# Weighted sum over experts: nine ring slots in chunks of three, one token of each chunk summed by TensorE in a loop, the code of three engines placed at instruction slot 128

## The chip, the cores and the metric

The kernel runs on one core of a Trainium2 chip. The metric is the device time of one execution in microseconds (us); lower is better. Before the change the median of three runs is 707.68 us, from 707.18 to 707.82.

A core has five engines with instruction queues of their own: TensorE (PE; its weight loads are listed apart as PEld), VectorE (DVE), ScalarE (ACT), GpSimd (POOL) and SyncE (SP). They meet only at semaphores. Transfers between the device memory and SBUF, the on-chip memory of 128 partitions, run on sixteen DMA engines; SP's DMAs stand in queue q1, ScalarE's in q10.

## The reference

```python
def setup_inputs():
    batch, seq, n_experts, expert_dim = 16, 1024, 8, 512
    return {
        "expert_outputs": np.random.randn(batch, seq, n_experts, expert_dim).astype(np.float32),
        "combine_weights": np.random.randn(batch, seq, n_experts).astype(np.float32),
    }

def reference(expert_outputs, combine_weights):
    weights = combine_weights[..., np.newaxis]
    return np.sum(expert_outputs * weights, axis=2).astype(np.float32)
```

Each of 16384 tokens has eight rows of 512 floats and eight weights; its output is the weighted sum of its rows. 268.4 MB are loaded and 33.6 MB stored, and each loaded value is used once.

## The kernel before

**Layout.** Tokens are spread over the 128 partitions, 128 tokens to a partition. "A token" in what follows means one token on every partition: 16 KB per partition or 2.097 MB to load, 2 KB per partition or 0.262 MB to store. 120 of the 128 go through a loop, in twelve rounds of ten; the last eight (the tail) go through code of their own.

**Buffers.** `ring` has ten token slots, filled in chunks of 4, 4 and 2 slots (`CHUNKS`). `acc` holds two halves of ten output tokens, one for even and one for odd rounds. `w_t` holds all weights, `w_c` those of two rounds.

**SP** (`loads_and_last_stores`) issues all loads of x (L101). A chunk of a round may be loaded again once `done`, a count of finished tokens, says that the chunk's tokens of the round before are summed (L99). The weights are loaded behind the first chunk (L105, L108). Behind the loop come eight loads of one tail token each (L111), then the last round's store (L91) and four stores of tail tokens of 4, 2, 1 and 1 tokens (L115).

**ScalarE** (`weights_and_stores`) issues the stores of the other rounds (L91), waits for each to land and then copies the weights of the round after next into `w_c` (L136). When the loop is over it writes diagonal matrices `diag`, the identity times one weight, for the tail (L143), five in flight.

**VectorE** (`terms`) does all sums of the loop. For a chunk it takes the semaphore `loaded` (L165), multiplies the first rows of all its tokens by their weights in one instruction (L189), then adds the other seven rows token by token in fused multiply-adds (L179), two tokens in turn, so that each instruction's wait on `step` for the one before it of the same token is covered by the other token's.

**TensorE** (`first_terms`) works only in the tail: for each of the eight tail tokens it sums the first four to six rows as products of a diagonal matrix with a row (L155), accumulating in PSUM; VectorE adds the remaining rows (L179 with `ps`), and for the last token both parts (L223, L230).

**GpSimd** writes the identity matrix at the start.

The order of the work is written out by hand: each engine runs its list in order, VectorE's loop of six iterations covers two rounds each, and no scheduler moves anything.

Of the kernel before, what the change touches and what calls it, by code (L numbers as in the profile page):

```python
# [10 lines left out]
def kernel(  # L11
# [17 lines left out]

    nc = tc.nc  # L30
    fp32 = mybir.dt.float32
    mult, add = mybir.AluOpType.mult, mybir.AluOpType.add

    B, S, E, D = expert_outputs.shape
    T = B * S
    P = 128
    R = 10
    G = 2 * R
    M = 2 * G
    T_P = T // P  # L40
    GROUPS = T_P // G
    LOOP = GROUPS * G
    TAIL = T_P - LOOP
    ROUNDS = LOOP // R
    CHUNKS = [(0, 4), (4, 4), (8, 2)]
    C = len(CHUNKS)
    DIAGS = 5

    x = expert_outputs.rearrange("b s e d -> (b s) e d")
    w = combine_weights.rearrange("b s e -> (b s) e")  # L50
    o = out.rearrange("b s d -> (b s) d")
    cut = LOOP * P
    x_g = x[0:cut].rearrange("(n p b g) e d -> n b p g e d", p=P, b=2, g=G)
    w_g = w[0:cut].rearrange("(n p m) e -> p n m e", p=P, m=M)
    o_g = o[0:cut].rearrange("(n p b g) d -> n b p g d", p=P, b=2, g=G)
    x_t = x[cut:T].rearrange("(p j) e d -> p j e d", j=TAIL)
    w_x = w[cut:T].rearrange("(p j) e -> p j e", j=TAIL)
    o_t = o[cut:T].rearrange("(p j) d -> p j d", j=TAIL)


    pe_e = [6, 6, 6, 6, 5, 5, 5, 4]
    tail_stores = [(0, 4), (4, 2), (6, 1), (7, 1)]
    diags = [(j, e) for j in range(TAIL) for e in range(pe_e[j])]
# [4 lines left out]
    acc = one.tile([P, G, D], fp32, name="acc")  # L68
    w_t = one.tile([P, T_P, E], fp32, name="w_t")
    w_c = one.tile([P, G, E], fp32, name="w_c")  # L70
    ident = one.tile([P, P], fp32, name="ident")
    diag = one.tile([P, DIAGS, P], fp32, name="diag")
    ps = psum.tile([P, TAIL, D], fp32, name="ps")

    sem = tc.alloc_semaphore
    w_in = sem("w_in")
    w_set = [sem(f"w_set{h}") for h in range(2)]
    loaded = [sem(f"loaded{c}") for c in range(C)]
    stored = [sem(f"stored{h}") for h in range(2)]
    step = sem("step")  # L80
    done = sem("done")
    tail_in = [sem(f"tail_in{j}") for j in range(TAIL)]
    tail_out = sem("tail_out")
    id_set = sem("id_set")
    diag_set = sem("diag_set")
    product = sem("product")

    def store(queue, n):
        h = n % 2
        queue.wait_ge(done, (n + 1) * R)  # L90
        queue.dma_start(  # L91
            out=o_g[n // 4, n // 2 % 2, :, h * R : h * R + R], in_=acc[:, h * R : h * R + R]
        ).then_inc(stored[h], 16)

    def loads_and_last_stores(sync):
        for n in range(ROUNDS):
            for c, (r, m) in enumerate(CHUNKS):
                if n:
                    sync.wait_ge(done, (n - 1) * R + r + m)  # L99
                g = n % 2 * R + r  # L100
                sync.dma_start(  # L101
                    out=ring[:, r : r + m], in_=x_g[n // 4, n // 2 % 2, :, g : g + m]
                ).then_inc(loaded[c], 16)
                if n == 0 and c == 0:
                    sync.dma_start(  # L105
                        out=w_t[:, 0:LOOP].rearrange("p (n m) e -> p n m e", m=M), in_=w_g
                    ).then_inc(w_in, 16)
                    sync.dma_start(out=w_t[:, LOOP:T_P], in_=w_x).then_inc(w_in, 16)  # L108
        for j in range(TAIL):
            sync.wait_ge(done, LOOP - R + j + 1)  # L110
            sync.dma_start(out=ring[:, j], in_=x_t[:, j]).then_inc(tail_in[j], 16)  # L111
        store(sync, ROUNDS - 1)
        for j, m in tail_stores:
            sync.wait_ge(done, LOOP + j + m)
            sync.dma_start(out=o_t[:, j : j + m], in_=acc[:, j : j + m]).then_inc(tail_out, 16)  # L115
# [13 lines left out]
    def weights_and_stores(scalar):  # L129
        scalar.wait_ge(w_in, 32)  # L130
        for n in range(ROUNDS):
            h = n % 2
            if n >= 2:
                store(scalar, n - 2)
                scalar.wait_ge(stored[h], 16 * (n // 2))
            scalar.copy(  # L136
                out=w_c[:, h * R : h * R + R], in_=w_t[:, n * R : n * R + R]
            ).then_inc(w_set[h], 1)
        store(scalar, ROUNDS - 2)
        scalar.wait_ge(stored[0], 16 * ROUNDS // 2)  # L140
        scalar.wait_ge(id_set, 2)
        for k, (j, e) in enumerate(diags):
            i = scalar.mul(out=diag[:, k % DIAGS], in_=ident, mul=w_t[:, LOOP + j, e : e + 1])  # L143
            i.then_inc(diag_set, 1)
            if k >= DIAGS:
                i.wait_op(product, k - DIAGS + 1, "sem-ge")
        scalar.wait_ge(stored[1], 16 * ROUNDS // 2)
        scalar.wait_ge(tail_out, 16 * len(tail_stores))

    def first_terms(tensor):  # L150
        for k, (j, e) in enumerate(diags):
            if e == 0:
                tensor.wait_ge(tail_in[j], 16)
            tensor.wait_ge(diag_set, k + 1)
            tensor.matmul(  # L155
                ps[:, j],
                lhsT=diag[:, k % DIAGS],
                rhs=ring[:, j, e],
                start=e == 0,
                stop=e == pe_e[j] - 1,  # L160
            ).then_inc(product, 1)

    def terms(vector):
        def take(s, v):
            vector.wait_ge(s, v).then_inc(s, -v)  # L165

        last = {}

        def count(i, g, e):

            if e == E - 1:
                i.then_inc(done, 1)
            else:
                i.then_inc(step, 1)
                last["all"] = last.get("all", 0) + 1
                last[g] = last["all"]

        def fused(g, e, weight, before):
            return vector.scalar_tensor_tensor(  # L179
                out=acc[:, g], in0=ring[:, g % R, e], scalar=weight, in1=before, op0=mult, op1=add  # L180
            )

        with nc.Fori(0, GROUPS, engines=OrderedEngineSet([vector.engine])):
            for h in range(2):
                take(w_set[h], 1)
                for c, (r, m) in enumerate(CHUNKS):
                    take(loaded[c], 16)
                    q = h * R + r
                    i = vector.tensor_tensor(  # L189
                        out=acc[:, q : q + m],  # L190
                        in0=ring[:, r : r + m, 0],
                        in1=w_c[:, q : q + m, 0:1].to_broadcast([P, m, D]),
                        op=mult,
                    )
                    i.then_inc(step, 1)
                    last["all"] = last.get("all", 0) + 1
                    last.update((g, last["all"]) for g in range(q, q + m))
                    for g in range(q, q + m, 2):
                        for e in range(1, E):
                            for k in (g, g + 1):  # L200
                                i = fused(k, e, w_c[:, k, e : e + 1], acc[:, k])
                                i.wait_op(step, last[k], "sem-ge")
                                count(i, k, e)
            take(step, last["all"])

        last.clear()
        for q in ((0, 1), (2,), (3,), (4,), (5,), (6,)):
            for e in range(pe_e[q[0]], E):
                for j in q:
                    weight = w_t[:, LOOP + j, e : e + 1]  # L210
                    if e == pe_e[j]:
                        i = fused(j, e, weight, ps[:, j])
                        i.wait_op(product, sum(pe_e[: j + 1]), "sem-ge")
                    else:
                        i = fused(j, e, weight, acc[:, j])
                        i.wait_op(step, last[j], "sem-ge")
                    count(i, j, e)

        j = TAIL - 1
        for e in range(pe_e[j], E):  # L220
            weight = w_t[:, LOOP + j, e : e + 1]
            if e == pe_e[j]:
                i = vector.tensor_scalar_mul(out=acc[:, j], in0=ring[:, j, e], scalar1=weight)  # L223
                i.wait_op(tail_in[j], 16, "sem-ge")
            else:
                i = fused(j, e, weight, acc[:, j])
                i.wait_op(step, last[j], "sem-ge")
            count(i, j, -1)
        vector.wait_ge(step, last[j])  # L229
        i = vector.tensor_tensor(out=acc[:, j], in0=acc[:, j], in1=ps[:, j], op=add)  # L230
        i.wait_op(product, len(diags), "sem-ge")
        count(i, j, E - 1)

    with tc.tile_critical(no_gpsimd_drain=True):  # L234
        loads_and_last_stores(nc.sync)
        identity(nc.gpsimd)
        weights_and_stores(nc.scalar)
        first_terms(nc.tensor)
        terms(nc.vector)
# [30 lines left out]
```

## Time and profile before

| | |
|---|---|
| median of three runs | 707.68 us |
| the profiled execution, its own time | 707.67 us |
| its span, first to last instruction | 705.5 us |
| granted TensorE clock, mean | 0.998 |
| moved by DMA | 302.53 MB, 429 GB/s over the span |
| VectorE busy | 642.8 us, 898 instructions |
| fused multiply-add, 128x512, with `w_c` | 840 of 745 ns each, which overlap a little |
| landing of a round's store of 2560 KB by ScalarE | 26.7 us median |
| landing of a chunk of two tokens, 4096 KB | 34.0 us median |
| ScalarE's first copy of weights starts | 24.39 us |

The profile is of one execution. Busy time is that of an engine's own instructions, without its waits. "Landing" runs from the issue of a DMA to its semaphore, so it includes the time that it stood in the queue. A line of the timeline has the start, the duration, the engine, the line of the code, the operation, output and inputs with their shapes, and in brackets the idle time before it and what ended it; an engine name with a q is its instruction queue, where it waits for semaphores. A line of busy time by stretches has the stretch, its length, and for each engine the busy time and in brackets the number of instructions, then the granted TensorE clock, the DMA share and GB/s.

### The profile page before, as it was taken

To read this page: it belongs to the slowest core of one execution; us is meant where nothing else is said; L and a number is where in the kernel's file an instruction comes from. 1 tells how busy PE (TensorE), PEld (TensorE's weight loads), DVE (VectorE), ACT (ScalarE), POOL (GpSimd) and SP (SyncE) were. 2 spreads that over 40 slices of the span, in tenths; PEclk is the share of its full clock that TensorE was granted. 3 is DMA by queue.
4 is the path that set the end of the run, shared out by engine and by line. 5 is a ranking of instruction groups with operands and counts; after the bars stand their busy time and mean duration, and the time that the engine had idled before them with its cause. 6 is when DMAs were issued, how large, how long until landed. Compare 5 with 4: busy or idle time off the path is not lost. (4 is left out here: it accounts for less than half of the span.)

```text
span 705.5 us, 1328 instructions
## 1 busy us (share of the span) xinstructions
PE 38.7 (5%) x86; PEld 16.9 (2%) x86; DVE 642.8 (91%) x898; ACT 21.1 (3%) x56; POOL 0.7 (0%) x6
## 2 busy tenths in 40 slices
PE   0000000000000000000000000000000000000695
PEld 0000000000000000000000000000000000000242
DVE  0599999979999989989999998998998998998964
ACT  0000000000000000000000000000000000000241
POOL 0000000000000000000000000000000000000000
PEclk9999999999999999999999999999999999999999
DMA  9999999999999999999999999999999999999997
GB/s 412 390 472 420 394 435 446 450 412 461 403 444 446 445 404 429 435 428 475 430 401 447 416 432 434 472 394 468 416 441 421 420 440 463 431 426 407 430 428 334
DMA packets 9186, 302.53 MB, mean 429 GB/s; under 512 B 1120, under 2 KB 1504, under 8 KB 1888
## 3 DMA queue, kind: packets, MB, share of 16 engines
q1 hardware_dynamic: 7600, 273.68, 90.0%
q10 hardware_dynamic: 1584, 28.84, 9.5%
q14 instruction: 2, 0.02, 0.0%
HBM read 268.96 MB, written 33.55 MB: 429 GB/s over the span
## 5 line engine op out<-in xcount | busy, mean ns | idle before, releaser
L179 DVE SCALAR_TENSOR_TENSOR acc<-ring,w_c,acc 128x512 f32<-128x512 f32 x840 | 559.7, 745 | 1.3
L189 DVE TENSOR_TENSOR acc<-ring,w_c 128x2048 f32<-128x2048 f32 (+1 forms) x36 | 69.5, 1931 | 46.2 <-DVEq L165 46.2
L155 PE MATMUL ps<-ring,diag 128*128 128x512 f32 x86 | 38.7, 613 | 659.1 <-DMA ring<-in_expert_outputs_dram 659.1
L155 PEld LDWEIGHTS ps<-ring,diag 128*128 128x128 f32 x86 | 16.9, 198 | 680.1 <-DMA ring<-in_expert_outputs_dram 659.1
L136 ACT COPY w_c<-w_t 128x80 f32<-128x80 f32 x12 | 3.0, 258 | 587.5 <-DMA out_dram<-acc 565.3
L143 ACT ACTIVATE diag<-ident,w_t 128x128 f32<-128x128 f32 x43 | 16.8, 400 | 84.4 <-DMA out_dram<-acc 54.2
L179 DVE SCALAR_TENSOR_TENSOR acc<-ring,w_t,ps 128x512 f32<-128x512 f32 x7 | 5.1, 744 | 9.6 <-PE ps L155 9.6
L179 DVE SCALAR_TENSOR_TENSOR acc<-ring,w_t,acc 128x512 f32<-128x512 f32 x13 | 9.7, 751 | 0.4
L136 ACT ACT_TABLE_LOAD x1 | 1.3, 1283 | 0.9 <-SPq L234 0.9
L230 DVE TENSOR_TENSOR acc<-acc,ps 128x512 f32<-128x512 f32 x1 | 0.7, 689 | 0.1
L223 DVE TENSOR_SCALAR acc<-ring,w_t 128x512 f32<-128x512 f32 x1 | 0.5, 481 | 0.0
L119 POOL TENSOR_SCALAR_AFFINE_SELECT ident<-ident 128x128 f32<-128x128 f32 x1 | 0.3, 292 | 0.1
L118 POOL MEMSET ident<- 128x128 f32 x1 | 0.2, 204 | 0.5 <-SPq L234 0.5
L254 POOL MEMSET const-bfloat16-1.0<- 128x1 bf16 x1 | 0.1, 101 | 0.0
L254 POOL MEMSET const-uint8-127<- 128x1 uint8 x1 | 0.1, 101 | 0.0
L254 POOL MEMSET const-float32-0.0<- 128x1 f32 x1 | 0.1, 98 | 0.2 <-issue 0.2
L254 POOL MEMSET const-float32-1.0<- 128x1 f32 x1 | 0.1, 98 | 0.0
## 6 DMA issues: line engine op xcount, KB each, us to landing
ring<-in_expert_outputs_dram SPq DMA_DIRECT2D x12, 4096.0 KB, 34.0
out_dram<-acc ACTq DMA_DIRECT2D x11, 2560.0 KB, 26.7
ring<-in_expert_outputs_dram SPq DMA_DIRECT2D x8, 2048.0 KB, 28.6
out_dram<-acc SPq DMA_DIRECT2D x1, 2560.0 KB, 24.8
out_dram<-acc SPq DMA_DIRECT2D x1, 1024.0 KB, 17.7
out_dram<-acc SPq DMA_DIRECT2D x1, 512.0 KB, 9.0
out_dram<-acc SPq DMA_DIRECT2D x2, 256.0 KB, 4.7
w_t<-in_combine_weights_dram SPq DMA_DIRECT2D x1, 480.0 KB, 22.6
```

The source lines that it names most:

```text
L118: gpsimd.memset(ident, 0.0).then_inc(id_set, 1)
L119: gpsimd.affine_select(out=ident, in_=ident, compare_op=mybir.AluOpType.not_equal, fill=1.0, base=0, pattern=[[-1, P]], channel_multiplier ...
L136: scalar.copy(out=w_c[:, h * R : h * R + R], in_=w_t[:, n * R : n * R + R]).then_inc(w_set[h], 1)
L143: i = scalar.mul(out=diag[:, k % DIAGS], in_=ident, mul=w_t[:, LOOP + j, e : e + 1])
L155: tensor.matmul(ps[:, j], lhsT=diag[:, k % DIAGS], rhs=ring[:, j, e], start=e == 0, stop=e == pe_e[j] - 1,).then_inc(product, 1)
L179: return vector.scalar_tensor_tensor(out=acc[:, g], in0=ring[:, g % R, e], scalar=weight, in1=before, op0=mult, op1=add)
L189: i = vector.tensor_tensor(out=acc[:, q : q + m], in0=ring[:, r : r + m, 0], in1=w_c[:, q : q + m, 0:1].to_broadcast([P, m, D]), op=mult,)
L223: i = vector.tensor_scalar_mul(out=acc[:, j], in0=ring[:, j, e], scalar1=weight)
L230: i = vector.tensor_tensor(out=acc[:, j], in0=acc[:, j], in1=ps[:, j], op=add)
L254: nc = _bacc.Bacc("TRN2", target_bir_lowering=False, num_devices=1)
```

## The change

- `ring` has nine slots, in three chunks of three. 126 tokens go through the loop, in fourteen rounds; two are left for the tail. `acc` has two halves of nine.
- Of each chunk VectorE sums the first two tokens as before. For the third it writes, in one instruction and ahead of its sums, eight diagonal matrices (identity times the token's eight weights, `diag`); TensorE, in a loop of fourteen iterations, multiplies them with the token's eight rows and accumulates in PSUM (`ps`), and ScalarE copies the sum to `acc`. A semaphore per chunk, `summed`, counts three finished tokens, two by VectorE and one by ScalarE; the loads and the stores wait on it.
- ScalarE issues the stores of all rounds but the last two, and copies the weights for round n + 1 after its second sum of round n, when the store of round n - 1 has landed.
- The tail: both tokens are loaded by SP when the first chunk of the last round is summed. The stores of the last two rounds stand behind them on SP's queue. VectorE writes their eight diagonals (four experts each) in one instruction after its loop, TensorE sums experts 0 to 3, VectorE adds 4 to 7, the two tokens in turn, and one DMA of 512 KB stores both.
- `head_slot` and `addr_align` place the loops of VectorE and TensorE and ScalarE's code so that they begin at instruction slot 128.
- The tokens that a load takes for one partition lie 63 tokens from those of the next partition (1008 KB) instead of 40 (640 KB); the number of bytes stays.

The diff, with removed runs of lines cut where the code above shows them:

```diff
-    R = 10
+    R = 9
+    C = 3
+    V = C - 1
     G = 2 * R
-    M = 2 * G
+    M = 7 * R
     T_P = T // P
-    GROUPS = T_P // G
-    LOOP = GROUPS * G
+    LOOP = T_P // M * M
     TAIL = T_P - LOOP
     ROUNDS = LOOP // R
-    CHUNKS = [(0, 4), (4, 4), (8, 2)]
-    C = len(CHUNKS)
-    DIAGS = 5
+    CHUNKS = R // C
+    HELD = 2
+    K = 4
+    BLOCK = 128
+    assert TAIL <= C and ROUNDS % 2 == 0
     x = expert_outputs.rearrange("b s e d -> (b s) e d")
     w = combine_weights.rearrange("b s e -> (b s) e")
     o = out.rearrange("b s d -> (b s) d")
     cut = LOOP * P
...
-    x_g = x[0:cut].rearrange("(n p b g) e d -> n b p g e d", p=P, b=2, g=G)
-    w_g = w[0:cut].rearrange("(n p m) e -> p n m e", p=P, m=M)
-    o_g = o[0:cut].rearrange("(n p b g) d -> n b p g d", p=P, b=2, g=G)
+    x_m = x[0:cut].rearrange("(n p k r) e d -> n k p r e d", p=P, k=M // R, r=R)
+    w_m = w[0:cut].rearrange("(n p m) e -> p n m e", p=P, m=M)
+    o_m = o[0:cut].rearrange("(n p k r) d -> n k p r d", p=P, k=M // R, r=R)
...
     ring = one.tile([P, R, E, D], fp32, name="ring")
     acc = one.tile([P, G, D], fp32, name="acc")
+    acc_t = one.tile([P, TAIL, D], fp32, name="acc_t")
     w_t = one.tile([P, T_P, E], fp32, name="w_t")
     w_c = one.tile([P, G, E], fp32, name="w_c")
     ident = one.tile([P, P], fp32, name="ident")
-    diag = one.tile([P, DIAGS, P], fp32, name="diag")
-    ps = psum.tile([P, TAIL, D], fp32, name="ps")
+    diag = one.tile([P, CHUNKS, E, P], fp32, name="diag")
+    diag_t = one.tile([P, TAIL, K, P], fp32, name="diag_t")
+    ps = psum.tile([P, CHUNKS, D], fp32, name="ps")
+    ps_t = psum.tile([P, TAIL, D], fp32, name="ps_t")
...
     def store(queue, n):
         h = n % 2
-        queue.wait_ge(done, (n + 1) * R)
+        queue.wait_ge(summed[-1], (n + 1) * C)
         queue.dma_start(
-            out=o_g[n // 4, n // 2 % 2, :, h * R : h * R + R], in_=acc[:, h * R : h * R + R]
+            out=o_m[n * R // M, n % (M // R)], in_=acc[:, h * R : h * R + R]
         ).then_inc(stored[h], 16)
 
     def loads_and_last_stores(sync):
         for n in range(ROUNDS):
-            for c, (r, m) in enumerate(CHUNKS):
+            for c in range(CHUNKS):
                 if n:
-                    sync.wait_ge(done, (n - 1) * R + r + m)
-                g = n % 2 * R + r
+                    sync.wait_ge(summed[c], n * C)
                 sync.dma_start(
-                    out=ring[:, r : r + m], in_=x_g[n // 4, n // 2 % 2, :, g : g + m]
+                    out=ring[:, c * C : c * C + C],
+                    in_=x_m[n * R // M, n % (M // R), :, c * C : c * C + C],
                 ).then_inc(loaded[c], 16)
                 if n == 0 and c == 0:
                     sync.dma_start(
-                        out=w_t[:, 0:LOOP].rearrange("p (n m) e -> p n m e", m=M), in_=w_g
+                        out=w_t[:, 0:LOOP].rearrange("p (n m) e -> p n m e", m=M), in_=w_m
                     ).then_inc(w_in, 16)
                     sync.dma_start(out=w_t[:, LOOP:T_P], in_=w_x).then_inc(w_in, 16)
+        sync.wait_ge(summed[0], ROUNDS * C)
         for j in range(TAIL):
-            sync.wait_ge(done, LOOP - R + j + 1)
             sync.dma_start(out=ring[:, j], in_=x_t[:, j]).then_inc(tail_in[j], 16)
-        store(sync, ROUNDS - 1)
-        for j, m in tail_stores:
-            sync.wait_ge(done, LOOP + j + m)
-            sync.dma_start(out=o_t[:, j : j + m], in_=acc[:, j : j + m]).then_inc(tail_out, 16)
+        for n in range(ROUNDS - HELD, ROUNDS):
+            store(sync, n)
+        sync.wait_ge(done, TAIL)
+        sync.dma_start(out=o_t, in_=acc_t).then_inc(tail_out, 16)
 
...
-    def weights_and_stores(scalar):
-        scalar.wait_ge(w_in, 32)
-        for n in range(ROUNDS):
+    def weights_sums_and_stores(scalar):
+        def weights(n):
             h = n % 2
-            if n >= 2:
-                store(scalar, n - 2)
-                scalar.wait_ge(stored[h], 16 * (n // 2))
             scalar.copy(
                 out=w_c[:, h * R : h * R + R], in_=w_t[:, n * R : n * R + R]
             ).then_inc(w_set[h], 1)
-        store(scalar, ROUNDS - 2)
-        scalar.wait_ge(stored[0], 16 * ROUNDS // 2)
+
+        scalar.addr_align(2 * BLOCK, offset=BLOCK, max_nops=0)
         scalar.wait_ge(id_set, 2)
-        for k, (j, e) in enumerate(diags):
-            i = scalar.mul(out=diag[:, k % DIAGS], in_=ident, mul=w_t[:, LOOP + j, e : e + 1])
...
+        scalar.wait_ge(w_in, 32)
+        weights(0)
+        weights(1)
+        for n in range(ROUNDS):
+            for c in range(CHUNKS):
+                i = scalar.copy(out=acc[:, n % 2 * R + c * C + V], in_=ps[:, c])
+                i.wait_op(product, (n * CHUNKS + c + 1) * E, "sem-ge").then_inc(summed[c], 1)
+                if c == 1 and 1 <= n < ROUNDS - 1:
+                    scalar.wait_ge(stored[(n - 1) % 2], 16 * ((n - 1) // 2 + 1))
+                    weights(n + 1)
+            if n < ROUNDS - HELD:
+                store(scalar, n)
+        for h in range(2):
+            scalar.wait_ge(stored[h], 16 * ROUNDS // 2)
+        scalar.wait_ge(tail_out, 16)
+
+    def take(engine, s, v):
+        engine.wait_ge(s, v).then_inc(s, -v)
+
+    def last_tokens(tensor):
+        def products(out, left_of, j, terms):
+            for e in range(terms):
+                tensor.matmul(
+                    out, lhsT=left_of[:, e], rhs=ring[:, j, e], start=e == 0, stop=e == terms - 1
+                ).then_inc(product, 1)
+
+        this = OrderedEngineSet([tensor.engine])
+        with nc.Fori(0, ROUNDS, engines=this, head_slot={tensor.engine: BLOCK}):
+            for c in range(CHUNKS):
+                take(tensor, fed, 1)
+                products(ps[:, c], diag[:, c], c * C + V, E)
+        tensor.wait_ge(fed, 1)
+        for j in range(TAIL):
+            tensor.wait_ge(tail_in[j], 16)
+            products(ps_t[:, j], diag_t[:, j], j, K)
 
     def terms(vector):
-        def take(s, v):
-            vector.wait_ge(s, v).then_inc(s, -v)
-
         last = {}
 
-        def count(i, g, e):
+        def count(i, g, e, end):
 
             if e == E - 1:
-                i.then_inc(done, 1)
+                i.then_inc(end, 1)
             else:
                 i.then_inc(step, 1)
                 last["all"] = last.get("all", 0) + 1
                 last[g] = last["all"]
 
-        def fused(g, e, weight, before):
+        def fused(out, x, weight, before):
             return vector.scalar_tensor_tensor(
-                out=acc[:, g], in0=ring[:, g % R, e], scalar=weight, in1=before, op0=mult, op1=add
+                out=out, in0=x, scalar=weight, in1=before, op0=mult, op1=add
             )
 
-        with nc.Fori(0, GROUPS, engines=OrderedEngineSet([vector.engine])):
+        this = OrderedEngineSet([vector.engine])
+        with nc.Fori(0, ROUNDS // 2, engines=this, head_slot={vector.engine: BLOCK}):
             for h in range(2):
-                take(w_set[h], 1)
-                for c, (r, m) in enumerate(CHUNKS):
...
+                take(vector, w_set[h], 1)
+                for c in range(CHUNKS):
+                    take(vector, loaded[c], 16)
+                    s = c * C
+                    g = h * R + s
+                    vector.tensor_tensor(
+                        out=diag[:, c],
+                        in0=ident[:, None, :].to_broadcast([P, E, P]),
+                        in1=w_c[:, g + V, :, None].to_broadcast([P, E, P]),
                         op=mult,
-                    )
-                    i.then_inc(step, 1)
+                    ).then_inc(fed, 1)
+                    vector.tensor_tensor(
+                        out=acc[:, g : g + V],
+                        in0=ring[:, s : s + V, 0],
+                        in1=w_c[:, g : g + V, 0:1].to_broadcast([P, V, D]),
+                        op=mult,
+                    ).then_inc(step, 1)
                     last["all"] = last.get("all", 0) + 1
-                    last.update((g, last["all"]) for g in range(q, q + m))
-                    for g in range(q, q + m, 2):
...
+                    last.update((k, last["all"]) for k in range(V))
+                    for e in range(1, E):
+                        for k in range(V):
+                            weight = w_c[:, g + k, e : e + 1]
+                            i = fused(acc[:, g + k], ring[:, s + k, e], weight, acc[:, g + k])
+                            i.wait_op(step, last[k], "sem-ge")
+                            count(i, k, e, summed[c])
+            take(vector, step, last["all"])
 
         last.clear()
-        for q in ((0, 1), (2,), (3,), (4,), (5,), (6,)):
-            for e in range(pe_e[q[0]], E):
...
+        vector.tensor_tensor(
+            out=diag_t,
+            in0=ident[:, None, None, :].to_broadcast([P, TAIL, K, P]),
+            in1=w_t[:, LOOP:T_P, 0:K, None].to_broadcast([P, TAIL, K, P]),
+            op=mult,
+        ).then_inc(fed, 1)
+        for e in range(K, E):
+            for j in range(TAIL):
+                weight = w_t[:, LOOP + j, e : e + 1]
+                if e == K:
+                    i = fused(acc_t[:, j], ring[:, j, e], weight, ps_t[:, j])
+                    i.wait_op(product, ROUNDS * CHUNKS * E + K * (j + 1), "sem-ge")
+                else:
+                    i = fused(acc_t[:, j], ring[:, j, e], weight, acc_t[:, j])
+                    i.wait_op(step, last[j], "sem-ge")
+                count(i, j, e, done)
 
```

More of the change, by code (lines that the diff above doesn't have):

```diff
@@ L58 @@
     o_t = o[cut:T].rearrange("(p j) d -> p j d", j=TAIL)
-    pe_e = [6, 6, 6, 6, 5, 5, 5, 4]
-    tail_stores = [(0, 4), (4, 2), (6, 1), (7, 1)]
-    diags = [(j, e) for j in range(TAIL) for e in range(pe_e[j])]
     one = ctx.enter_context(tc.tile_pool(name="one", bufs=1))
@@ L77 @@
     w_set = [sem(f"w_set{h}") for h in range(2)]
-    loaded = [sem(f"loaded{c}") for c in range(C)]
+    loaded = [sem(f"loaded{c}") for c in range(CHUNKS)]
     stored = [sem(f"stored{h}") for h in range(2)]
@@ L81 @@
     done = sem("done")
+    fed = sem("fed")
+    product = sem("product")
+    summed = [sem(f"summed{c}") for c in range(CHUNKS)]
     tail_in = [sem(f"tail_in{j}") for j in range(TAIL)]
@@ L84 @@
     id_set = sem("id_set")
-    diag_set = sem("diag_set")
-    product = sem("product")
     def store(queue, n):
         h = n % 2
-        queue.wait_ge(done, (n + 1) * R)
+        queue.wait_ge(summed[-1], (n + 1) * C)
         queue.dma_start(
-            out=o_g[n // 4, n // 2 % 2, :, h * R : h * R + R], in_=acc[:, h * R : h * R + R]
+            out=o_m[n * R // M, n % (M // R)], in_=acc[:, h * R : h * R + R]
         ).then_inc(stored[h], 16)
@@ L138, in weights_and_stores @@
             ).then_inc(w_set[h], 1)
-        store(scalar, ROUNDS - 2)
-        scalar.wait_ge(stored[0], 16 * ROUNDS // 2)
+        scalar.addr_align(2 * BLOCK, offset=BLOCK, max_nops=0)
         scalar.wait_ge(id_set, 2)
-        for k, (j, e) in enumerate(diags):
[L143 to L161, printed above, removed]
+        scalar.wait_ge(w_in, 32)
@@ L184, in terms @@
             for h in range(2):
-                take(w_set[h], 1)
-                for c, (r, m) in enumerate(CHUNKS):
[L187 to L192, printed above, removed]
-                        op=mult,
-                    )
-                    i.then_inc(step, 1)
-                    last["all"] = last.get("all", 0) + 1
-                    last.update((g, last["all"]) for g in range(q, q + m))
-                    for g in range(q, q + m, 2):
[L199 to L203, printed above, removed]
@@ L204, in terms @@
-            take(step, last["all"])
-        last.clear()
-        for q in ((0, 1), (2,), (3,), (4,), (5,), (6,)):
-            for e in range(pe_e[q[0]], E):
[L209 to L230, printed above, removed]
@@ L231, in terms @@
-        i.wait_op(product, len(diags), "sem-ge")
-        count(i, j, E - 1)
+                take(vector, w_set[h], 1)
[7 more added lines that the diff above has]
+                        in1=w_c[:, g + V, :, None].to_broadcast([P, E, P]),
+                        op=mult,
+                    ).then_inc(fed, 1)
[5 more added lines that the diff above has]
+                    ).then_inc(step, 1)
+                    last["all"] = last.get("all", 0) + 1
+                    last.update((k, last["all"]) for k in range(V))
[5 more added lines that the diff above has]
+                            count(i, k, e, summed[c])
@@ L236 @@
         identity(nc.gpsimd)
-        weights_and_stores(nc.scalar)
-        first_terms(nc.tensor)
+        weights_sums_and_stores(nc.scalar)
+        last_tokens(nc.tensor)
         terms(nc.vector)
```

## The prediction

> **What bounds the kernel now.** I read the page's busy shares first, then its DMA queues, then the busy time by stretches of the span, the order of instructions through one round, and last the chain of waits.
>
> ```profile
> PE 38.7 (5%) x86; PEld 16.9 (2%) x86; DVE 642.8 (91%) x898; ACT 21.1 (3%) x56; POOL 0.7 (0%) x6
> ...
> DMA  9999999999999999999999999999999999999997
> ...
> q1 hardware_dynamic: 7600, 273.68, 90.0%
> q10 hardware_dynamic: 1584, 28.84, 9.5%
> q14 instruction: 2, 0.02, 0.0%
> ```
>
> VectorE is busy 91% of the span, but the sixteen DMA engines are busy all of it: 90.0% + 9.5%. The loads (q1, mostly descriptors of 64 and 32 KB) move 3.04 MB per per cent of share and the stores (q10, descriptors of 20 KB) 3.04 as well, so descriptor size costs nothing visible between 20 and 64 KB.
>
> ```profile
> 239.05:293.48 54.43, 0.00 (x0) 0.00 (x0) 52.26 (x74) 0.26 (x1) 0.00 (x0) 1.00 1.00 433
> ...
> 565.63:620.06 54.43, 0.00 (x0) 0.00 (x0) 52.27 (x74) 0.26 (x1) 0.00 (x0) 1.00 1.00 433
> ...
> 701.00:702.00 1.00, 0.00 (x0) 0.00 (x0) 0.00 (x0) 0.00 (x0) 0.00 (x0) 1.00 0.88 334
> 702.00:703.00 1.00, 0.00 (x0) 0.00 (x0) 0.00 (x0) 0.00 (x0) 0.00 (x0) 1.00 0.12 47
> ```
>
> The last two columns are DMA share and GB/s; the one with 52.26 is VectorE. Every round of ten tokens takes 54.43 us with DMA share 1.00. Ten tokens are 10 x (2.097 loaded + 0.262 stored) = 23.59 MB, so 433.4 GB/s. All 302.53 MB at that rate are 698.0 us of the 705.5 us span, and data still flows at 702. Nothing of size is left to win: the kernel is a DMA stream from start to end.
>
> ```profile
> 282.95 1.22 DVE L189 TENSOR_TENSOR acc<-ring,w_c 128x1024 f32<-128x1024 f32 x1
> 284.21 9.37 DVE L179 SCALAR_TENSOR_TENSOR acc<-ring,w_c,acc 128x512 f32<-128x512 f32 x14
> 293.49 2.29 DVE L189 TENSOR_TENSOR acc<-ring,w_c 128x2048 f32<-128x2048 f32 x1
> ...
> 316.49 2.29 DVE L189 TENSOR_TENSOR acc<-ring,w_c 128x2048 f32<-128x2048 f32 x1 [2.04 <-DVEq L165]
> ```
>
> VectorE waits about 2.06 us in each round for the middle chunk; otherwise it keeps up. The first two rows give my VectorE prices: two tokens cost 10.54 us (282.95 to 293.49), one 128x1024 product 1.25 with its gap, fourteen alternating sums 9.29, so 0.665 each.
>
> **The change, in the loop.** VectorE does, per chunk of three, one 128x1024 product that writes eight diagonals (1.25; both its operands are broadcast, which no row shows; the bounds are 0.69, the 128x512 addition at L230, and 2.29, the 128x2048 product; I take 1.25, equal shape) and two tokens (10.54): 11.8 us, 35.4 per round. DMA per round is 0.9 x 54.43 = 49.0 us. VectorE therefore drops from almost equal to DMA to 72% of it, and its 2.06 us waits grow to some 13.6 us a round. That is worth nothing, because DMA is what it waits for.
>
> TensorE's eight products per chunk: in the old tail each product leaves two matmul records.
>
> ```profile
> 660.96 0.34 PEld L155 LDWEIGHTS ps<-ring,diag 128*128 128x128 f32 x1 [0.52 <-issue]
> 661.81 0.34 PEld L155 LDWEIGHTS ps<-ring,diag 128*128 128x128 f32 x1 [0.52 <-ACT diag L143]
> 662.48 0.19 PEld L155 LDWEIGHTS ps<-ring,diag 128*128 128x128 f32 x1 [0.33 <-issue]
> 662.91 0.19 PEld L155 LDWEIGHTS ps<-ring,diag 128*128 128x128 f32 x1 [0.24 <-issue]
> ```
>
> Spacing is 0.85 us for the first 3.4 us after 659.09 and 0.43 afterwards (the granted clock reads 1.00 there all the same). Sixteen records are 6.5 + 0.6 for the last = 7.1 us at the fast spacing, 8.7 from a cold start, 13.6 if none speeds up. Even the last is ready by 1.25 + 13.6 plus ScalarE's copy (a 128x512 copy out of PSUM is not in the trace: between 0.26, its 128x80 copy, and 0.75, VectorE's read of ps; I take 0.75) = 15.6 us. A ring slot comes back 12 to 16 us after it lands; two other chunks, 2 x 14.5 us of loads, are queued then. DMA starves only beyond 29 us. If that cover went, each chunk would cost the excess.
>
> ScalarE now queues copies behind its wait for a store of the round before: 8 descriptor pairs of 48 and 18 KB per engine, scaled by size from the 26.7 us of today's 64 and 20 KB, some 21 us; it asks 32 us after issue, so no copy is held. SP's queue: loads wait on `summed`, the last two stores move from ScalarE to SP behind the two tail loads, whose wait (first chunk of the last round done) ends 17 us before the last chunk lands. Bytes are unchanged; the start gains nothing (weights land 4.8 us sooner, while DMA runs on through a ring that holds 43 us).
>
> **The change, at the end.** Here order matters. First, when does the last chunk of the loop land (L)? Today the second chunk of the last round lets VectorE go at 643.09. By then 118 tokens, the weights, ten stores and 22.9/26.7 of the eleventh have moved: 276.4 MB, 637.8 us at 433.4 GB/s. The lead is 5.3 us. After the change 126 tokens, weights and twelve stores precede L: 293.0 MB = 676.1 us, so L = 681.4.
>
> Behind L come two tail tokens, two stores, 8.91 MB or 20.6 us: DMA runs out of work at 702.0, as today. But today everything is then stored. After the change a serial chain starts at L:
> - last chunk on VectorE, 0.1 + 11.8, since its diagonals and two tokens precede everything of the tail;
> - one product for the tail's diagonals, 1.25 (bounds as above; twice on this chain, so -1.1 to +2.1 in all);
> - TensorE's eight tail products, 7.1 to 8.7; TensorE was idle some 3.0 us (its last chunk ends at L + 1.35 + 8.7, the chain reaches it at L + 13.15), while the row shows a start after 659 us of idleness. I take 7.9;
> - the second token's first sum waits for the eighth product; it and six more sums take 6 x 0.665 + 0.75 = 4.75;
> - the store of 512 KB. Today's last store took 3.9 us to land for 256 KB; 0.6 more for the bytes, 4.5, and 0.1 to issue;
> - from that landing to the end of the span, 705.5 - 704.2 = 1.3.
>
> Sum 31.7, so a span of **713.1**. The profiled execution took 707.67 with a span of 705.5, and the median is 707.68; I add 2.2: **715.3 us**, 7.6 (1.1%) more than now. Today the end is spread differently: eight tail tokens arrive while TensorE has been at them for 35 us, and the last store is 256 KB:
>
> ```profile
> 659.09 35.33 PE ps L155 x78
> ...
> 698.77 0.76 DVE acc L179
> 699.53 0.03 issue
> 699.56 0.02 DVEq L229
> 699.58 0.05 issue
> 699.63 0.69 DVE acc L230
> ```
>
> VectorE ends at 700.3 now and at 707.3 by my sum.
>
> [...]
>
> Code: the three loops are moved to slot 128. Today VectorE's loop of over 146 instructions passes its back edge with no gap in the records, and q14 fetched two packets in the whole run. I cost code loading at 0; the upper bound, on leaving a loop, is one 48 KB packet ahead of it (1.8 us at 27.1 GB/s per engine) and a landing like the smallest store's 3.9: 5.7.
>
> **Rivals.**
> - TensorE never speeds up (13.6 per eight products). Its last chunk ends at L + 15.0, the tail's at L + 28.6 instead of L + 21.05: 722.8 us. For it: bursts with pauses. Against: the old tail sped up within 3.4 us. 6%.
> - The load stream slows: partition rows of the loads lie 1008 KB apart instead of 640, which no run shows. Each per cent lost is 6.8 us; at one per cent 722. The old tail loads, 128 KB apart, ran at 419 to 438. 5%.
> - Code loading stalls at the exit of VectorE's or TensorE's loop: up to 721. 4%.
> - **Not slower:** DMA speeds up because VectorE leaves SBUF alone for a quarter of its time. It decides from L = 673.8, that is 293.0 MB in 668.5 us, 438.3 GB/s; at 440 the time is 705.1. For it: VectorE's busy time falls by 140 us. Against: share 1.00 and the same 433 in every round, and no better rate in the first 24 us, when VectorE did nothing (415, the lead included). 5%.
>
> [...]
>
> **How the numbers follow.** The forecast has 80%: 715.3, its own range 712.5 to 718 from the diagonals' and TensorE's bounds. Stretching to part of the code and stream cases above and of a faster stream below gives 711.5 to 719.5. This measurement tells 0.2% (1.4 us) from no change; the fourth rival gives faster 0.04 and, with the forecast's far edge, same 0.02; the rest, 0.94, is slower.
>
> **What would show it.** Rounds of 49.0 us at 433 GB/s; VectorE near 510 us busy with waits for loads in every chunk; DMA idle from about 702 until one last store issued near 707; TensorE's tail products after VectorE's last loop sum. Wrong if the last store is issued before 703, if rounds differ from 49.0 by over 0.3, or if TensorE's eight products take over 10 us.

## The result, and the profile after

The changed kernel takes 713.39 us (median of six runs, 712.87 to 715.59) against 707.57 for the kernel before on the same chips: a ratio of 1.0086, 95% interval 1.0072 to 1.0100. The forecast was 715.3 with a range of 711.5 to 719.5. The profiled execution took 712.98 us with a span of 710.4.

The page of the changed kernel first, its busy times and DMA queues:

```profile
PE 400.8 (56%) x688; PEld 163.8 (23%) x688; DVE 499.1 (70%) x681; ACT 28.1 (4%) x57; POOL 0.7 (0%) x6
...
q1 hardware_dynamic: 7184, 274.21, 89.5%
q10 hardware_dynamic: 1728, 28.31, 9.3%
q14 instruction: 2, 0.02, 0.0%
```

VectorE is busy 144 us less than before and TensorE 362 us more, and the load and store queues still take 98.8% of a span that is 4.9 us longer. The number of instruction packets (q14) is the same two.

Busy time by stretches of the changed kernel, two rounds from the middle and single microseconds from the end; DMA share and GB/s stand last, the granted TensorE clock before them:

```profile
280.50:329.50 49.00, 28.95 (x48) 11.70 (x48) 35.21 (x49) 1.91 (x4) 0.00 (x0) 0.74 1.00 433
476.50:525.50 49.00, 28.32 (x48) 11.47 (x48) 35.18 (x48) 1.91 (x4) 0.00 (x0) 0.78 1.00 433
...
701.00:702.00 1.00, 0.78 (x2) 0.00 (x0) 0.18 (x1) 0.00 (x0) 0.00 (x0) 1.00 0.13 55
702.00:703.00 1.00, 0.00 (x0) 0.00 (x0) 1.00 (x2) 0.00 (x0) 0.00 (x0) 1.00 0.00 0
...
707.00:708.00 1.00, 0.00 (x0) 0.00 (x0) 0.00 (x0) 0.00 (x0) 0.00 (x0) 0.50 0.62 250
```

A round of nine tokens takes 49.0 us at 433 GB/s (VectorE starts on the first chunks of two successive rounds at 280.51 and 329.47), nine tenths of the 54.43 us that ten took: the loop is the same DMA stream as before. VectorE is busy 35.2 us of it and waits for the rest. The difference is at the end: from 702 DMA stands still and VectorE is at work, and at 707 DMA moves the last 0.52 MB.

The chain of waits of the changed kernel (start, duration, what) names no DMA at all; before, a load and TensorE's long tail were in it. First the load of the kernel before, then the changed kernel:

```profile
631.12 27.93 DMA ring<-in_expert_outputs_dram
```

```profile
681.69 1.23 DVE diag L202
682.92 1.15 DVE acc L208
...
684.09 8.11 DVE acc L190 x13
...
693.46 1.15 DVE diag_t L225
694.60 0.04 issue
694.65 7.15 PE ps_t L163 x16
...
701.82 4.72 DVE acc_t L190 x7
```

Read it downwards: the last chunk of the loop lands, VectorE works through it, writes the tail's diagonals, TensorE takes 7.15 us, VectorE 4.72. None of these steps overlaps the next. The list of DMA issues of the changed kernel (size, us from issue to landing) has the last link:

```profile
out_dram<-acc_t SPq DMA_DIRECT2D x1, 512.0 KB, 2.6
```

### The profile page after: what moved, and what is told of

Read it like the earlier page. It is cut to its first block, busy times and chain, and to the rows that moved or that the text cites. A ratio compares the mean times of both kernels' runs of the same rounds, so it can differ in the third digit from the quotient of the medians.

```text
span 710.4 us, 2392 instructions
## 1 busy us (share of the span) xinstructions
PE 400.8 (56%) x688; PEld 163.8 (23%) x688; DVE 499.1 (70%) x681; ACT 28.1 (4%) x57; POOL 0.7 (0%) x6
## 5 line engine op out<-in xcount | busy, mean ns | idle before, releaser
L163 PE MATMUL ps<-ring,diag 128*128 128x512 f32 x672 | 393.6, 752 | 298.6 <-PEq L158 298.6
L190 DVE SCALAR_TENSOR_TENSOR acc<-ring,w_c,acc 128x512 f32<-128x512 f32 x588 | 393.3, 747 | 1.5
L163 PEld LDWEIGHTS ps<-ring,diag 128*128 128x128 f32 x672 | 160.8, 247 | 530.6 <-issue 530.6
L202 DVE TENSOR_TENSOR diag<-ident,w_c 128x1024 f32<-128x1024 f32 x42 | 51.5, 1225 | 199.5 <-DVEq L158 199.5
L208 DVE TENSOR_TENSOR acc<-ring,w_c 128x1024 f32<-128x1024 f32 x42 | 51.2, 1218 | 0.0
L146 ACT COPY acc<-ps 128x512 f32<-128x512 f32 x42 | 24.6, 585 | 644.4 <-PE ps L163 644.4
L163 PE MATMUL ps_t<-ring,diag_t 128*128 128x512 f32 x16 | 7.1, 599 | 2.4 <-DVE diag_t L225 2.4
L163 PEld LDWEIGHTS ps_t<-ring,diag_t 128*128 128x128 f32 x16 | 3.0, 190 | 6.6 <-issue 3.3
L190 DVE SCALAR_TENSOR_TENSOR acc_t<-ring,w_t,acc_t 128x512 f32<-128x512 f32 x6 | 4.1, 746 | 0.0
L135 ACT COPY w_c<-w_t 128x72 f32<-128x72 f32 x14 | 3.5, 254 | 0.0
L135 ACT ACT_TABLE_LOAD x1 | 1.3, 1283 | 20.4 <-DMA w_t<-in_combine_weights_dram 20.4
```

Of the source, the lines that this page charges most:

```text
L135: scalar.copy(out=w_c[:, h * R : h * R + R], in_=w_t[:, n * R : n * R + R]).then_inc(w_set[h], 1)
L146: i = scalar.copy(out=acc[:, n % 2 * R + c * C + V], in_=ps[:, c])
L163: tensor.matmul(out, lhsT=left_of[:, e], rhs=ring[:, j, e], start=e == 0, stop=e == terms - 1).then_inc(product, 1)
L190: return vector.scalar_tensor_tensor(out=out, in0=x, scalar=weight, in1=before, op0=mult, op1=add)
L202: vector.tensor_tensor(out=diag[:, c], in0=ident[:, None, :].to_broadcast([P, E, P]), in1=w_c[:, g + V, :, None].to_broadcast([P, E, P]), ...
L208: vector.tensor_tensor(out=acc[:, g : g + V], in0=ring[:, s : s + V, 0], in1=w_c[:, g : g + V, 0:1].to_broadcast([P, V, D]), op=mult,).the ...
```

## The experiments

My theory: the loop costs what its bytes cost at 433 GB/s, whatever the engines do in it, and the time is the landing of the loop's last chunk plus a serial chain behind it. Rivals: code loading, all bytes alone setting the end, VectorE's relief being worth something in the loop, VectorE slowing DMA.

**The change without the placement.** `e1_no_slots`, and again beside the change itself on one chip:

```diff
-        scalar.addr_align(2 * BLOCK, offset=BLOCK, max_nops=0)
...
-        with nc.Fori(0, ROUNDS, engines=this, head_slot={tensor.engine: BLOCK}):
+        with nc.Fori(0, ROUNDS, engines=this):
...
-        with nc.Fori(0, ROUNDS // 2, engines=this, head_slot={vector.engine: BLOCK}):
+        with nc.Fori(0, ROUNDS // 2, engines=this):
```

> The changed kernel without the placement at slot 128 for all three engines. Theory (the loop is the DMA stream's, code loading costs nothing): 713.4 us within 1, span 710.4, rounds 49.0 us. Rival (without the placement the loops' back edges load code): a gap at each of VectorE's seven back edges; if it is longer than the 2.8 to 8.8 us that VectorE waits for loads anyway, rounds above 49.0 and more than 715 us.

Measured 712.26 us (712.16 to 713.61), a ratio of 1.0067 (1.0050 to 1.0084). That is 1.1 us below the 713.4 that I had given within 1, so both kernels ran again side by side:

> The changed kernel itself, on one chip with the next one. Theory: 713 us; its runs fall on spans near 710.4 or near 712.1, since TensorE's eight tail products take 7.15 us at full clock or some 1.7 more when the pause before them lowers it.

> The changed kernel without the placement at slot 128, as before, beside the change on one chip. Theory (code loading costs nothing): the same two spans, 710.4 and near 712, and a median within 1 us of the change's. Rival (the placement matters): a difference of more than 1.5 us whose place is a gap behind a back edge or at a loop's exit.

Measured 712.56 us for the change (ratio 1.0070, 1.0056 to 1.0083) and 712.18 without the placement (1.0066, 1.0052 to 1.0080). The medians differ by 0.4 us and the intervals of the ratios overlap; all five spans of the change lay between 710.0 and 710.4, all five without the placement between 710.3 and 710.6. From the first to the last instruction the placement is worth nothing here. The 0.4 us lie outside the span: the nine executions without the placement took 1.75 to 1.82 us more than their span, the eleven with it 2.1 to 3.5. No run shows what takes that time.

The longer span that I expected now and then appeared in none of these ten, but once in each of the earlier sets: 712.1 in one execution of the change, 711.8 in the profiled one of `e1_no_slots`. Only the second has a profile. Its place is shown by TensorE's tail, of the change first and of `e1_no_slots` below it, and by two stretches of `e1_no_slots`:

```profile
694.65 7.13 PE L163 MATMUL ps_t<-ring,diag_t 128*128 128x512 f32 x16 [2.41 <-DVE diag_t L225]
```

```profile
694.31 8.83 PE L162 MATMUL ps_t<-ring,diag_t 128*128 128x512 f32 x16 [1.93 <-DVE diag_t L224]
...
694.00:696.00 2.00, 1.69 (x3) 0.80 (x4) 0.25 (x1) 0.00 (x0) 0.00 (x0) 0.67 0.99 424
696.00:698.00 2.00, 2.00 (x4) 0.84 (x3) 0.00 (x0) 0.00 (x0) 0.00 (x0) 0.50 1.01 433
```

The granted clock is 0.67 and 0.50 there, and in the second stretch four matmul records fit into 2 us, where the change has six at 1.00. TensorE's eight tail products take 8.85 us by the chain instead of 7.15. In that execution the longer span is these 1.7 us, beside a lower clock, and no gap at a loop's exit; that the 712.1 is the same is likely, but no profile shows it.

**A store moved ahead of the last loads.** `e2_held_one`:

```diff
-    HELD = 2
+    HELD = 1
```

> The changed kernel with HELD = 1: the store before the last is issued by ScalarE at once and moves ahead of the last loads, bytes unchanged. Theory (the time is the landing of the last loop chunk plus a serial chain): that chunk lands 2.36 MB / 433.4 GB/s = 5.4 us later, 687.1 instead of 681.7, span 715.8, 718.8 us. Rival (the end is set by all bytes through DMA): no change, 713.4 us.

Measured 718.04 us (ratio 1.0156, 1.0139 to 1.0173), span 715.9. Its chain of waits:

```profile
687.10 1.22 DVE diag L202
...
700.05 7.15 PE ps_t L163 x16
...
707.22 4.72 DVE acc_t L190 x7
```

Every link is as long as before, and all start 5.4 us later. No byte was added; 2.36 MB changed places with the last loads, and the end moved by as much as they take. So the end is not set by the sum of bytes, but by what stands ahead of the last chunk. (One of its four executions has a span of 717.6, 1.8 above the others.)

**The tail on VectorE alone.** `e3_tail_vector` drops the tail's diagonals and its products on TensorE:

```diff
-        vector.tensor_tensor(
-            out=diag_t,
...
+        vector.tensor_tensor(
+            out=acc_t,
+            in0=ring[:, 0:TAIL, 0],
+            in1=w_t[:, LOOP:T_P, 0:1].to_broadcast([P, TAIL, D]),
+            op=mult,
+        ).then_inc(step, 1)
...
+        for e in range(1, E):
+            for j in range(TAIL):
+                weight = w_t[:, LOOP + j, e : e + 1]
+                i = fused(acc_t[:, j], ring[:, j, e], weight, acc_t[:, j])
```

> The changed kernel with both tail tokens summed by VectorE alone, all eight experts, no diagonals and no TensorE behind the loop. Theory (serial chain behind the last chunk): 1.15 + 7.15 + 4.75 us leave the chain and 10.5 (one 128x1024 product and fourteen sums) enter, so 2.5 less: VectorE ends at 704.0 instead of 706.5, span 707.9, 710.9 us. Rival (TensorE's share of the tail shortens the end, or the last store alone sets it): 713.4 us or more.

Measured 709.72 us (ratio 1.0033, 1.0021 to 1.0046), span 707.7, 2.7 less than the change. The end of its chain:

```profile
693.29 1.14 DVE acc_t L221
694.43 0.03 issue
694.46 9.36 DVE acc_t L184 x14
```

VectorE sums both tokens from 693.3 to 703.8. The way through a second engine, 1.15 + 7.15 + 4.72 = 13.0, is longer than the 10.5 of doing the work at home: for half of the rows the diagonals and TensorE cost 8.3, VectorE by itself 10.5 - 4.7 = 5.8, and since the two engines take turns, nothing of it is hidden.

**No TensorE in the loop.** `e4_all_vector` gives VectorE the third token of each chunk too (the diagonals of the loop and the placement of its own loop go with it):

```diff
-    V = C - 1
+    V = C
...
-            for c in range(CHUNKS):
-                take(tensor, fed, 1)
-                products(ps[:, c], diag[:, c], c * C + V, E)
...
-                i = scalar.copy(out=acc[:, n % 2 * R + c * C + V], in_=ps[:, c])
```

> The changed kernel with all three tokens of each chunk on VectorE, TensorE only in the tail. Theory: 15.8 us per chunk, 47.4 per round, still under 49.0, so rounds stay 49.0 and the last chunk lands at 681.7; only the last chunk's sums are 4.1 us longer, and TensorE starts the tail cold, 1.5 to 2.5 more: span 716.0 to 717.0, 719 us. Rival (VectorE's relief in the loop is worth time there): rounds above 49.5 us, the last chunk 7 us or more later, 725 us or more.

Measured 721.37 us (ratio 1.0200, 1.0183 to 1.0217), span 719.8: 2.4 us over what I expected, and below the rival. By stretches, the last nine tokens with a wait in them and the nine after them, up to the last chunk:

```profile
588.80:637.79 48.99, 0.00 (x0) 0.00 (x0) 47.19 (x66) 0.25 (x1) 0.00 (x0) 1.00 1.00 433
637.79:684.91 47.12, 0.00 (x0) 0.00 (x0) 47.01 (x66) 0.00 (x0) 0.00 (x0) 1.00 1.00 430
```

The first is 49.0 us long like the two rounds before it: with VectorE at 47.2 us the loop keeps its pace, and the relief is worth nothing there. In the second VectorE does not wait at all. I had overlooked that the last two stores are held back: without a store a chunk lands every 14.5 us and VectorE needs 15.7, so it falls behind and starts the last chunk at 684.9, 3.2 us late. Then the last chunk takes 15.7 us instead of 11.7, and TensorE, idle until then, 9.3 for the tail instead of 7.2. 3.2 + 4.0 + 2.1 = 9.3, and the span is 9.4 longer. TensorE's share of each chunk pays here at the end of the loop only.

**Few sums.** `e5_few_sums` leaves out the fused sums of the loop, seven of each eight products of TensorE, and three of four experts of the tail on either engine; every transfer and wait stays:

```diff
-                products(ps[:, c], diag[:, c], c * C + V, E)
+                products(ps[:, c], diag[:, c], c * C + V, 1)
...
-                    ).then_inc(step, 1)
-                    last["all"] = last.get("all", 0) + 1
...
+                    ).then_inc(summed[c], V)
```

> The changed kernel with most sums left out: VectorE adds only each first row, TensorE one row of the third token, the tail one row on each; all loads, stores and waits stay. Theory (DMA is full at its own rate whatever the engines do): rounds 49.0 us, last chunk lands at 681.7, DMA ends at 702, span 704.3, 706.8 us: the floor of this order of transfers. Rival (DMA is slowed by VectorE's use of SBUF): rounds under 48.7 us and a span under 700.

Measured 706.59 us (ratio 0.9988, 0.9979 to 0.9998), span 704.8. Its busy times and the landing of its last store, and the start of its last chunk in the timeline:

```profile
PE 90.0 (13%) x88; PEld 22.0 (3%) x88; DVE 101.8 (14%) x87; ACT 28.1 (4%) x57; POOL 0.7 (0%) x6
...
out_dram<-acc_t SPq DMA_DIRECT2D x1, 512.0 KB, 9.2
```

```profile
681.75 1.22 DVE L202 TENSOR_TENSOR diag<-ident,w_c 128x1024 f32<-128x1024 f32 x1 [12.18 <-DVEq L158]
```

VectorE is busy 14% of the span, rounds run at the same 433 GB/s, and the last chunk starts at 681.75, as in the change (681.69). DMA did not run faster beside a VectorE that was mostly idle. 706.6 us is what this order of transfers costs with hardly any sums, its floor, 0.9 us below the kernel before.

**A shorter chain.** `e6_short_tail` writes the tail's diagonals before the loop, lets TensorE go at the tail tokens as soon as its last chunk is done, has VectorE do its own experts first and add TensorE's sums last, and stores each tail token by itself:

```diff
+        vector.wait_ge(w_set[0], 1)
+        vector.tensor_tensor(
+            out=diag_t,
...
+        ).then_inc(fed_t, 1)
         this = OrderedEngineSet([vector.engine])
...
+        for j in range(TAIL):
+            vector.wait_ge(step, last[j])
+            i = vector.tensor_tensor(out=acc_t[:, j], in0=acc_t[:, j], in1=ps_t[:, j], op=add)
...
+            sync.wait_ge(done, j + 1)
+            sync.dma_start(out=o_t[:, j], in_=acc_t[:, j]).then_inc(tail_out, 16)
```

> The changed kernel with the chain behind the last chunk shortened: the tail's diagonals are written before the loop, TensorE sums the tail while VectorE is at the last chunk, VectorE does its own four experts first and adds TensorE's sums last, and each tail token has its own store. Theory: VectorE ends at 681.7 + 18.4 = 700.1, before DMA is through at 702; span 704.2, 706.8 us, some 6.5 less than the change and at most 0.8 below the kernel before. Rival (something else than that chain holds the end): over 710 us.

Measured 707.06 us (ratio 0.9994, 0.9985 to 1.0004), span 705.0. In its timeline TensorE's two last blocks now touch, beside VectorE's sums:

```profile
683.04 10.10 PE L165 MATMUL ps<-ring,diag 128*128 128x512 f32 x16 [5.75 <-PEq L160]
...
692.99 7.03 PE L165 MATMUL ps_t<-ring,diag_t 128*128 128x512 f32 x16
...
700.05 0.69 DVE L252 TENSOR_TENSOR acc_t<-acc_t,ps_t 128x512 f32<-128x512 f32 x1 [0.79 <-PE ps_t L165]
```

The chain's end falls from 706.5 to 700.7, where I had 700.1, and the loss is gone. How much of it each of the four edits brings is not shown. The result cannot be told from the kernel before: its interval holds 1. With the floor 0.1% under the kernel before, no kernel here that does all sums beats it.

## Why the prediction was right

- **The loop.** Forecast 49.0 us per round at 433 GB/s and the last chunk at 681.4; measured 49.0, 433 and 681.7. `e5_few_sums` and `e4_all_vector` show why nothing that VectorE gains there counts.
- **Loads in rows 1008 KB apart, code at slot 128.** Both were put at nothing, and inside the span both are: a round runs at 433 GB/s before and after, and side by side the spans without the placement are 710.3 to 710.6 against 710.0 to 710.4. Those two rivals fall.
- **The start.** "The start gains nothing" held, but not as told: of the 4.8 us that the weights should land sooner, VectorE got 2.7 (22.2 instead of 24.9). They landed 20.4 us after the start, 4.0 sooner, and then ScalarE's table load of 1.28 us, at 0.9 us before and behind the wait for the weights now, stood ahead of the copy. DMA ran on meanwhile, at 393 GB/s from 20 to 22 and 467 from 22 to 24.
- **The chain.** From the landing on, forecast and measured: last chunk 11.8 and 11.7; diagonals 1.25 and 1.28; TensorE 7.9 and 7.2; VectorE's last sums 4.75 and 4.7; the last store's issue and landing 4.6 and 2.6; to the end of the span 1.3 and 1.2. One instruction that writes diagonals, which no row had shown with both operands broadcast, takes 1.22 us, as the 128x1024 product of the kernel before does.
- **The terms of the sum.** The span came out at 710.4 instead of 713.1. Two terms were too large. The store's is the larger, by 1.9 us: I took 3.9 us for 256 KB from the kernel before as the price of a store by itself. But between its issue at 700.3 and 702 DMA moved some 0.6 MB (397 GB/s up to 701, then the 334 of the row that I showed), of which 0.26 were its own: that store had queued behind another, and the store of twice the size into empty queues landed in 2.6. `e5_few_sums` shows the same from the other side: the same 512 KB, issued at 694.3 behind two held stores, took 9.2. TensorE's term was 0.7 too large: I took the middle between 7.1 at the fast spacing and 8.7 from a start like the one after 659 us of idleness, and it came out at the first.
- **Luck.** The median missed by 1.9 us and the span by 2.7. The 2.2 that I added for the time outside the span were 2.2 to 3.5 in the six executions of the change, so an error there hid part of the other two; it is also why the loss reads 5.8 us here and 5.0 in `e7_change_again`, with spans alike. And the lower end of my own range, 712.5, does not come from its bounds, and no run shows it: 715.3 - 1.1 - 0.8 is 713.4, which is what was measured, with rounds at 433 GB/s and the last chunk's start at 681.7.
- **The clock.** In the profiled execution of the change the tail's products after a pause of 2.4 us began at the fast spacing, at a granted clock of 1.00; in that of `e1_no_slots`, after 1.9 us, they lost it. There the clock reads 1.00 from 692 to 694, 0.67 over the next two microseconds and 0.50 from 696 to 698; with a single step from 1.00 to 0.50 the 0.67 puts it near 694.7 (an estimate), after the products had begun at 694.31. The shorter of the two pauses is the one with the lower clock behind it, so a longer pause is not what tells the two apart, and no run shows what does. A longer span was rare; 10 of the 11 spans of the change lie at 710.0 to 710.7.
- **TensorE never speeding up** fell: within the loop eight products took 8.5 to 10.2 us, not 13.6. But my 8.7 from a cold start was low: they took 9.4 on average, since the slow spacing of 0.85 us could outlast the 3.4 us that I had read in the kernel before (in the block that starts at 36.25 it went on to about 42). Six of the 42 took over 10 us, which I had named as a sign of being wrong without saying which eight. It cost nothing in the loop, where rounds stayed at 49.0 us; the tail's eight took 7.15.
- **Not slower because DMA speeds up** fell by `e5_few_sums`: with VectorE busy 14% of the span, rounds ran at the same 433 GB/s.

## What to carry to other kernels

When DMA share is 1.00 in every round and the rate does not move from round to round (433 GB/s here), relief for a compute engine in the loop bought nothing here; look at what stands ahead of the last load and at what has to follow it. Behind the last landing each step counted in full here: the tail took 13.0 us through two engines in turn and 10.5 on VectorE alone, and the span was 2.7 shorter with the second (710.4 and 707.7). So split work there over engines only where they run at the same time. One store of 2.36 MB ahead of the last loads made the span 5.5 us longer (715.9), so look for transfers that can be held behind the last load. And a landing time is a price only together with the state of the queue at its issue: 512 KB took 2.6 us into idle queues and 9.2 behind two stores.

## What the hardware showed that was not expected

- TensorE's granted clock reads 0.50 over the first microsecond of 40 of the 42 bursts of the loop, which last 9.4 us on average with pauses of 4.4 to 11.4 us between them (one of 3.2), and its mean over the kernel is 0.78; the burst length swings between 8.5 and 10.2 us with the same work. In the kernel before, the same slow spacing of 0.85 us at TensorE's first products (659 to 662) stood beside a granted clock of 1.00, and so it did in the first burst of the change (23.57), so the spacing of the records is the safer reading.
- A DMA of 512 KB into idle queues landed 2.6 us after its issue, less than the 3.9 us of one of 256 KB behind a queue that was still draining, and than the 9.2 us of one of 512 KB behind two stores of 2304 KB.
